# Tree attention on one core: reordered first loads, first scores and V copies

## Chip, cores, metric

One core of a Trainium2 chip. The metric is the device time of one execution in microseconds (us); the span in a profile (first to last instruction) is about 1.8 us shorter. Each kernel ran several times. A run is called fast or slow by the spread of the runs of its kernel (slow: more than 1.5% above the fastest); comparisons use fast runs where they can, and the text says where a profile is of a slow run. Ratios are the mean time of one kernel's fast runs over that of the other's of the same rounds, so they are not quite the ratios of the medians quoted beside them.

## The reference

```python
batch, heads, seq, dim = 8, 12, 512, 64
# mask[i, j] = 1 where j is i or an ancestor of i in a binary heap of 512 nodes
scores = np.einsum('bhqd,bhkd->bhqk', Q, K) / np.sqrt(dim) + (1 - mask) * (-1e9)
weights = np.exp(scores - scores.max(-1, keepdims=True))
weights = weights / (weights.sum(-1, keepdims=True) + 1e-10)
out = np.einsum('bhqk,bhkd->bhqd', weights, V)
```

The kernel computes only the tiles of the score matrix in which the mask has ones.

## The kernel before

96 heads are worked in 48 pairs. Loads come by quad (four heads, two pairs), issued from GpSimd's queue, and arrive as bf16. V is then copied into a permuted layout, one `vt` tile per octet (eight heads, four pairs): `spread_top` runs on GpSimd, `spread_l7` and `spread_leaves` on VectorE. VectorE and GpSimd run their instructions in program order in the traces here (the prediction shows a normalisation held for 7.23 us behind a copy that waits).

```python
def spread_top(o, h0=0, h1=8):        # 4 copies on GpSimd (L193)
def spread_leaves(o, r, h0=0, h1=8):  # 1 copy on VectorE (L201); r = 0, 1
def spread_l7(o, quad, h0=0, h1=8):   # 1 copy on VectorE (L213); quad = 0..3
# ... cut ...
psO = ctx.enter_context(tc.tile_pool(name="psO", bufs=1, space=bass.MemoryType.PSUM))
# ... cut ...
load(0, 2)                            # K twice, Q twice, V
load(1)
spread_top(0, 0, 4)
load(2)
spread_top(0, 4, 8)
load(3)
for i in range(2):
    transpose(i)
    evac(i)
# ... octet 0's copies on VectorE, cut ...
loaded, stored = 4, 0
for i in range(NP + 1):               # NP = 48
    q, r = divmod(i, 2)
    scores1(i)
    values(i - 1, 0)                  # guards on i cut
    scores2(i)
    values(i - 1, 1)
    norm(i - 1)                       # VectorE (L339, L340); frees the one ob tile
    transpose(i + 2)
    evac(i + 2)                       # VectorE (L253)
    o = i // 4 + 1
    if o < NQ // 2:
        if i % 4 == 0:
            spread_top(o)
        if i % 4 < 2:
            spread_l7(o, 2 * (i % 4))
            spread_l7(o, 2 * (i % 4) + 1)
        else:
            spread_leaves(o, i % 4 - 2)
    if loaded < min(NQ, q + 1 + AHEAD):
        load(loaded)
        loaded += 1
```

`values(i - 1, a)` is a run of matmuls for one head: first four that need only the top copies (L316), then two (L321) and four (L327) that need the leaves and l7 copies. They all write the tile `ob`, of which there is one. Octet `o` is first used by pair `4*o`, that is by `values` in iteration `4*o + 1`.

The softmax here doesn't subtract the row's maximum and nothing guards it: scores larger than these inputs give would overflow.

Of the kernel before, what the change touches and what calls it, by code (L numbers as in the profile page):

```python
# [34 lines left out]
def _slot_layout(t):  # L35

    found = sorted((_psum_unit(u), ROWS[kind]) for u, (kind, s) in enumerate(UNITS) if s == t)
    return [r for _, r in found], [u for u, _ in found]
# [58 lines left out]
def kernel(  # L97
# [7 lines left out]
    nc = tc.nc  # L105
    B, H, S, D = Q.shape
    P = nc.NUM_PARTITIONS
    assert S == 512 and D == 64 and P == 128 and (B * H) % 4 == 0
    scale = float(1.0 / np.sqrt(D))
    NQ = B * H // 4  # L110
    NP = 2 * NQ

    fp32 = mybir.dt.float32
    bf16 = mybir.dt.bfloat16
# [3 lines left out]
    Qr = Q.rearrange("b h (p t) d -> p (b h) (t d)", t=4)  # L118
    Kr = K.rearrange("b h (p t) d -> p (b h) (t d)", t=4)
# [9 lines left out]
    loads = ctx.enter_context(tc.tile_pool(name="loads", bufs=8))  # L129
# [34 lines left out]
    qsts, ksts, vsts = {}, {}, {}  # L164
    qTs, kTs, kqps, obs, ets, ofs = {}, {}, {}, {}, {}, {}

    def load_one(name, kept, src, q, parts=1):
        st = loads.tile([P, 4, 4, D], bf16, name=name)
        n = 4 // parts
        for j in range(parts):  # L170
            nc.gpsimd.dma_start(  # L171
                out=st[:, n * j:n * j + n, :, :].rearrange("p h t d -> p h (t d)"),
                in_=src[:, 4 * q + n * j:4 * q + n * j + n, :],
            )
        kept[q] = st

    def load_v(q):
        o, half = divmod(q, 2)
        if half == 0:
            vsts[o] = vloads.tile([P, 8, 4, D], bf16, name="vst")  # L180
        nc.gpsimd.dma_start(  # L181
            out=vsts[o][:, 4 * half:4 * half + 4, :, :].rearrange("p h t d -> p h (t d)"),
            in_=Vr[:, 4 * q:4 * q + 4, :],
        )

    def load(q, parts=1):
        load_one("kst", ksts, Kr, q, parts)
        load_one("qst", qsts, Qr, q, parts)
        load_v(q)

    def spread_top(o, h0=0, h1=8):
        for j in range(4):
            nc.gpsimd.tensor_copy(  # L193
                out=vts[o % NV][32 * j:32 * j + 32, h0:h1, 0, 0:D],
                in_=vsts[o][0:32, h0:h1, UNITS[TOP + j][1], :],
            )

    def spread_leaves(o, r, h0=0, h1=8):

        p = 64 if r else 0  # L200
        nc.vector.tensor_copy(  # L201
            out=vts[o % NV][p:p + 64, h0:h1, 1 + r:4 + r:2, 0:D],
            in_=vsts[o][64:128, h0:h1, r:3 + r:2, :],
        )

    def spread_l7(o, quad, h0=0, h1=8):

        first, slot, step = ((2, 0, 3), (2, 2, -1), (1, 3, -3), (1, 1, 1))[quad]
        src = vsts[o][32:64, h0:h1, slot, :]
        src = bass.AP(  # L210
            src.tensor, src.offset, [list(src.ap[0]), list(src.ap[1]), [step * D, 2], [1, D]]
        )
        nc.vector.tensor_copy(  # L213
            out=vts[o % NV][32 * quad:32 * quad + 32, h0:h1, first:first + 3:2, 0:D], in_=src
        )

    def transpose_one(dst, i, a, t, units, st, perm):

        step = units[1] - units[0]
        if units[2] - units[1] == step:  # L220
            dst = dst[64 * a:64 * a + 64, units[0]:units[3] + 1:step, :]
        else:
            gap = units[2] - units[0]
            dst = dst[64 * a:64 * a + 64, units[0]:units[0] + 2 * gap, :].rearrange(
                "p (x y) c -> p x y c", x=2
            )[:, :, 0:2, :]
        nc.tensor.transpose(  # L227
            out=dst, in_=st[i // 2][:, 2 * (i % 2) + a, t, :], identity=perm
        )

    def transpose(i):
        kqp = psT.tile([P, 2, 32, 32], bf16, name="kqp")
        kqps[i] = kqp
        for t in range(4):
            for a in range(2):
                transpose_one(kqp[:, 0, :, :], i, a, t, _slot_layout(t)[1], ksts, perms[t])
        for t in range(4):
            for a in range(2):
                transpose_one(
                    kqp[:, 1, :, :], i, a, t, [2 * t, 2 * t + 1, 2 * t + 9, 2 * t + 10],  # L240
                    qsts, qperm,
                )

    def evac(i):
        kq = work.tile([P, 2, 16, 32], bf16, name="kq")
        kTs[i] = kq[:, 0, :, :]
        qTs[i] = kq[:, 1, :, :].rearrange("p (t u) c -> p t (u c)", t=4)
        src = kqps[i][:, :, 0:18, :]
        src = bass.AP(
            src.tensor, src.offset,  # L250
            [list(src.ap[0]), [1024, 2], [32, 8], [9 * 32, 2], [1, 32]],
        )
        nc.vector.tensor_copy(  # L253
            out=kq[:, :, :, :].rearrange("p k (x y) c -> p k x y c", y=2), in_=src
        )
# [4 lines left out]
    def scores1(i):  # L260

        sp = psS.tile([P, 2, 512], fp32, name="s1")
        for a in range(2):
            nc.tensor.matmul(  # L264
                out=sp[:, a, :], lhsT=k1code[64 * a:64 * a + 64, :],
                rhs=q1code[64 * a:64 * a + 64, :], start=True, stop=False,
            )
        for a in range(2):
            nc.tensor.matmul(  # L269
                out=sp[:, a, :], lhsT=keys(i, a, TOP),  # L270
                rhs=qTs[i][64 * a:64 * a + 64, :, :].rearrange("p t c -> p (t c)"),
                start=False, stop=True,
            )
        et = etpool.tile([P, 2, 4, 128], bf16, name="e1")
        nc.scalar.activation(  # L275
            out=et[:, :, :, :].rearrange("p a t c -> p (a t c)"),
            in_=sp[:, :, :].rearrange("p a c -> p (a c)"),
            func=AF.Exp, scale=scale,
        )
        ets[i] = et  # L280
# [25 lines left out]
    def values(i, a):  # L306
        hh = 2 * (i % 4) + a
        if a == 0:
            obs[i] = psO.tile([P, 2, 512], fp32, name="ob")
        ob, e1, e2, vt = obs[i], ets[i], e2s[i % NE], vts[(i // 4) % NV]  # L310

        def o(t, lo=0, hi=128):
            return ob[lo:hi, a, 65 * t:65 * t + 65]

        for t in range(4):
            nc.tensor.matmul(  # L316
                out=o(t), lhsT=e1[:, a, t, :], rhs=vt[:, hh, 0, 0:D + 1],
                start=t == 0, stop=False,
            )
        for t in (2, 3):  # L320
            nc.tensor.matmul(  # L321
                out=o(t), lhsT=e2[:, a, t, :], rhs=vt[:, hh, 1 + t, 0:D + 1],
                start=False, stop=False,
            )
        for t in (0, 1):
            for lo, tile2 in ((0, SELF[t]), (64, t)):
                nc.tensor.matmul(  # L327
                    out=o(t, lo, lo + 64), lhsT=e2[:, a, t, lo:lo + 64],
                    rhs=vt[:, hh, 1 + tile2, 0:D + 1],
                    start=False, stop=t == 1,  # L330
                )
# [21 lines left out]
    AHEAD = 6  # L353
    BEHIND = 6

    load(0, 2)
    load(1)
    spread_top(0, 0, 4)
    load(2)
    spread_top(0, 4, 8)  # L360
    load(3)
    for i in range(2):
        transpose(i)
        evac(i)
    for h in (0, 4):
        for r in range(2):
            spread_leaves(0, r, h, h + 4)
        for j in range(4):
            spread_l7(0, j, h, h + 4)

    loaded, stored = 4, 0
    for i in range(NP + 1):
        q, r = divmod(i, 2)
        if i < NP:
            scores1(i)
        if 1 <= i <= NP:
            values(i - 1, 0)
        if i < NP:
            scores2(i)
        if 1 <= i <= NP:  # L380
            values(i - 1, 1)
            norm(i - 1)
        if i + 2 < NP:
            transpose(i + 2)
            evac(i + 2)
        o = i // 4 + 1
        if o < NQ // 2:
            if i % 4 == 0:
                spread_top(o)
            if i % 4 < 2:  # L390
                spread_l7(o, 2 * (i % 4))
                spread_l7(o, 2 * (i % 4) + 1)
            else:
                spread_leaves(o, i % 4 - 2)
        if loaded < min(NQ, q + 1 + AHEAD):
            load(loaded)
            loaded += 1
        behind = BEHIND if loaded < NQ else 0
        if stored < NQ - 1 and 2 * (stored + behind) + 3 <= i and (r == 1 or loaded == NQ):
            store(nc.gpsimd, stored)  # L400
            stored += 1
        if i == NP - 1:
            store(nc.sync, NQ - 1, 0, 2)
# [33 lines left out]
```

## Time and profile before

| | |
|---|---|
| median of the runs taken with the change | 161.43 us (160.22 to 163.19, 5 runs) |
| span of the profile | 159.7 us, mean granted TensorE clock 0.959 |
| first scores of pair 7 begin | 45.08 us |
| first scores of pair 47 begin | 150.25 us |
| so 40 pairs of the steady stage | 105.17 us, 2.63 each |

The start of pair 7's first scores is used below as the end of the ramp. The stretch from there to pair 47's is called the steady stage. The lines of the profile that carry the argument are in the prediction.

### The profile page before, as it was taken

The page shows a single profiled execution, that of the slowest core. Times are in us where ns is not written, and L with a number is a line of the kernel's source. Part 1 is how long each engine was busy: PE and PEld are TensorE (multiplying, and loading weights), DVE is VectorE, ACT ScalarE, POOL GpSimd, SP SyncE. Part 2 cuts the span into 40 slices and gives each one's busy share as a digit, 9 for nine tenths or more (in the row PEclk, how much of TensorE's full clock was granted, in tenths as well). Part 3 has the DMA queues.
Part 4 walks back from the last instruction along what each step waited for, and adds up shares of the span by engine and source line. Part 5 has one row for each costly group of instructions (what it writes and reads, how often), then busy time and mean ns, then how long its engine had stood idle before and what let it go on. Part 6 is the DMA issues. An engine that isn't in the chain of part 4 may idle for free.

```text
span 159.7 us, 5887 instructions
## 1 busy us (share of the span) xinstructions
PE 127.2 (80%) x2592; PEld 82.7 (52%) x2592; DVE 113.0 (71%) x229; ACT 89.0 (56%) x98; POOL 104.2 (65%) x153
## 2 busy tenths in 40 slices
PE   0378702995499899899999898999999989899860
PEld 0244301663366556565657565656657665566540
DVE  1065307671947998978889889798898998886621
ACT  3033310466046667666768576657768676567720
POOL 7839607993967979987977969669759780111010
PEclk9999999999659999999999999999999999999975
DMA  4999990999999999999999999999999999521351
GB/s 134 143 172 149 164 143 1 114 174 195 196 197 196 198 199 189 197 251 224 255 266 248 228 253 264 253 228 252 263 248 240 383 390 359 190 80 55 135 197 68
DMA packets 42090, 32.30 MB, mean 202 GB/s; under 512 B 1616, under 2 KB 38992, under 8 KB 42064
## 3 DMA queue, kind: packets, MB, share of 16 engines
q0 software_dynamic: 41360, 30.94, 109.0%
q1 hardware_dynamic: 560, 0.85, 1.6%
q8 instruction: 20, 0.33, 0.8%
q10 hardware_dynamic: 144, 0.13, 0.2%
q14 instruction: 6, 0.05, 0.1%
HBM read 38.21 MB, written 12.58 MB: 318 GB/s over the span
## 4 chain that ended last, share of the span: by engine, by line
PE 51%; DVE 19%; DMA 13%; POOL 10%; issue 4%; DVEq 0%; POOLq 0%
DMA vst<-in_V_dram 13%; PE ob L316 12%; PE ob L327 9%; PE kqp L227 8%; DVE of L340 8%; DVE vt L213 6%; PE s L286 6%; PE s L264 5%; PE s L295 4%; POOL vt L193 4%; PE s L269 4%; PE ob L321 3%; POOL kst L171 3%; POOL qst L171 3%; DVE kq L253 3%
## 5 line engine op out<-in xcount | busy, mean ns | idle before, releaser
L275 ACT ACTIVATE e<-s 128x1024 bf16<-128x1024 f32 x48 | 49.1, 1023 | 45.6 <-PE s L269 45.6
L300 ACT ACTIVATE e<-s 128x768 bf16<-128x768 f32 x48 | 38.9, 810 | 17.9 <-PE s L295 16.3
L316 PE MATMUL ob<-vt,e 128*128 128x65 bf16 x384 | 29.1, 200 | 18.2 <-DVE of L340 15.7
L193 POOL COPY vt<-vst 32x512 bf16<-32x512 bf16 (+1 forms) x52 | 31.8, 612 | 17.6 <-DMA vst<-in_V_dram 13.2
L316 PEld LDWEIGHTS <-e 128*128 128x128 bf16 x384 | 17.6, 100 | 44.9 <-DVE of L340 31.7
L253 DVE COPY kq<-kqp 128x1024 bf16<-128x1024 bf16 x48 | 32.7, 682 | 7.4 <-PE kqp L227 7.4
L213 DVE COPY vt<-vst 32x1024 bf16<-32x1024 bf16 (+1 forms) x52 | 27.2, 524 | 11.5 <-DMA vst<-in_V_dram 10.4
L340 DVE TENSOR_TENSOR of<-ob,rec 128x512 f32<-128x512 f32 x48 | 33.2, 691 | 1.7
L348 POOL DMA_DIRECT2D out_dram<-of x23 | 17.5, 761 | 22.4 <-DVE of L340 18.0
L227 PE MATMUL kqp<-ctile,kst 128*64 128x128 bf16 x384 | 20.3, 230 | 8.0 <-DMA kst<-in_K_dram 5.8
L327 PE MATMUL ob<-vt,e 128*64 128x65 bf16 x384 | 24.9, 212 | 0.0
L339 DVE RECIPROCAL rec<-ob 128x8 f32<-128x8 f32 x48 | 10.0, 208 | 19.2 <-PE ob L327 18.4
L321 PE MATMUL ob<-vt,e 128*128 128x65 bf16 x192 | 22.2, 198 | 0.0
L227 PE MATMUL kqp<-ctile,qst 128*64 128x128 bf16 x384 | 20.5, 231 | 2.0 <-DMA qst<-in_Q_dram 1.9
L171 POOL DMA_DIRECT2D qst<-in_Q_dram x25 | 19.0, 760 | 2.9 <-PE ob L316 1.7
L181 POOL DMA_DIRECT2D vst<-in_V_dram x24 | 18.6, 774 | 2.9 <-DMA vst<-in_V_dram 1.7
L171 POOL DMA_DIRECT2D kst<-in_K_dram x25 | 19.0, 759 | 2.0 <-POOLq L421 0.8
L264 PE MATMUL s<-ctile 64*128 64x512 bf16 x96 | 19.9, 409 | 0.0
L269 PE MATMUL s<-kq 64*128 64x512 bf16 x96 | 19.5, 401 | 0.0
L295 PEld LDWEIGHTS <-kq 64*128 64x128 bf16 x576 | 16.8, 97 | 3.9 <-issue 1.1
L227 PEld LDWEIGHTS <-kst 128*64 128x64 bf16 x384 | 13.7, 117 | 8.5 <-DMA kst<-in_K_dram 6.0
L295 PE MATMUL s<-kq 64*128 64x64 bf16 (+2 forms) x576 | 18.0, 193 | 0.0
(17 smaller groups left out, 88.0 us busy)
## 6 DMA issues: line engine op xcount, KB each, us to landing
out_dram<-of POOLq DMA_DIRECT2D x23, 512.0 KB, 9.5
vst<-in_V_dram POOLq DMA_DIRECT2D x24, 256.0 KB, 9.4
kst<-in_K_dram POOLq DMA_DIRECT2D x23, 256.0 KB, 8.0
qst<-in_Q_dram POOLq DMA_DIRECT2D x23, 256.0 KB, 8.6
ctile<-tree_consts SPq DMA_DIRECT2D x1, 448.0 KB, 3.1
kst<-in_K_dram POOLq DMA_DIRECT2D x2, 128.0 KB, 3.9
qst<-in_Q_dram POOLq DMA_DIRECT2D x2, 128.0 KB, 4.4
out_dram<-of SPq DMA_DIRECT2D x1, 256.0 KB, 2.2
```

The source lines that it names most:

```text
L171: nc.gpsimd.dma_start(out=st[:, n * j:n * j + n, :, :].rearrange("p h t d -> p h (t d)"), in_=src[:, 4 * q + n * j:4 * q + n * j + n, :],)
L193: nc.gpsimd.tensor_copy(out=vts[o % NV][32 * j:32 * j + 32, h0:h1, 0, 0:D], in_=vsts[o][0:32, h0:h1, UNITS[TOP + j][1], :],)
L213: nc.vector.tensor_copy(out=vts[o % NV][32 * quad:32 * quad + 32, h0:h1, first:first + 3:2, 0:D], in_=src)
L227: nc.tensor.transpose(out=dst, in_=st[i // 2][:, 2 * (i % 2) + a, t, :], identity=perm)
L253: nc.vector.tensor_copy(out=kq[:, :, :, :].rearrange("p k (x y) c -> p k x y c", y=2), in_=src)
L264: nc.tensor.matmul(out=sp[:, a, :], lhsT=k1code[64 * a:64 * a + 64, :], rhs=q1code[64 * a:64 * a + 64, :], start=True, stop=False,)
L275: nc.scalar.activation(out=et[:, :, :, :].rearrange("p a t c -> p (a t c)"), in_=sp[:, :, :].rearrange("p a c -> p (a c)"), func=AF.Exp, s ...
L295: nc.tensor.matmul(out=sp[:, a, t, lo:hi], lhsT=keys(i, a, TILE2[tile2]), rhs=qTs[i][64 * a:64 * a + 64, t, lo:hi], start=False, stop=(t, ...
L300: nc.scalar.activation(out=e2s[i % NE][:, :, :, 32:128].rearrange("p a t c -> p (a t) c"), in_=sp[:, :, :, 32:128].rearrange("p a t c -> p ...
L316: nc.tensor.matmul(out=o(t), lhsT=e1[:, a, t, :], rhs=vt[:, hh, 0, 0:D + 1], start=t == 0, stop=False,)
L327: nc.tensor.matmul(out=o(t, lo, lo + 64), lhsT=e2[:, a, t, lo:lo + 64], rhs=vt[:, hh, 1 + tile2, 0:D + 1], start=False, stop=t == 1,)
L340: nc.vector.tensor_tensor(out=ofs[q][:, 2 * r:2 * r + 2, :, :], in0=o4[:, :, :, 0:D], in1=rec[:, :, :, :].to_broadcast([P, 2, 4, D]), op=A ...
```

## The change

Its intent: the first K and Q halves and V arrive sooner, the first scores don't wait for pair 1's transposes, and octet 1's copies no longer hold up the normalisations on VectorE and the loads on GpSimd. To get that, the copies of octets 1 to 11 move two iterations later (the second leaves copy one iteration), and both leaves copies share one iteration. Core of the diff (the helper `load_one` gives way to `load_qk`, not shown):

```diff
-    load(0, 2)
+    load_qk(0, 2)                # half of K, half of Q, V, half of K, half of Q
     load(1)
     spread_top(0, 0, 4)
     load(2)
     spread_top(0, 4, 8)
-    load(3)
-    for i in range(2):
-        transpose(i)
-        evac(i)
+    transpose(0)
+    evac(0)
 ... octet 0's copies: half of them here, the other half in iterations 0 and 1
-        if i + 2 < NP:
-            transpose(i + 2)
-            evac(i + 2)
-        o = i // 4 + 1
-        if o < NQ // 2:
-            if i % 4 == 0:
-                spread_top(o)
-            if i % 4 < 2: ...two spread_l7
-            else:
-                spread_leaves(o, i % 4 - 2)
-        if loaded < min(NQ, q + 1 + AHEAD):
+        for n in ([1, 2] if i == 0 else [i + 2]):
+            if n < NP:
+                transpose(n)
+                evac(n)
+        o = (i - 2) // 4 + 1
+        step = (i - 2) % 4
+        if i >= 2 and o < NQ // 2 and step == 0:
+            ...spread_top(o), by halves for o == 1
+        if loaded < min(NQ, i + 4, q + 1 + AHEAD):
             load(loaded)
             loaded += 1
+        if i >= 2 and o < NQ // 2:
+            if step < 2: ...two spread_l7
+            elif step == 2:
+                spread_leaves(o, 0)
+                spread_leaves(o, 1)
```

In the changed kernel the lines are numbered four higher: L197 are GpSimd's top copies, L205 the leaves, L217 the l7 copies, L257 the evacuation, L320, L325 and L331 the value matmuls, L343 and L344 the normalisation.

More of the change, by code (lines that the diff above doesn't have):

```diff
@@ L165 @@
     qTs, kTs, kqps, obs, ets, ofs = {}, {}, {}, {}, {}, {}
-    def load_one(name, kept, src, q, parts=1):
-        st = loads.tile([P, 4, 4, D], bf16, name=name)
-        n = 4 // parts
-        for j in range(parts):
-            nc.gpsimd.dma_start(
-                out=st[:, n * j:n * j + n, :, :].rearrange("p h t d -> p h (t d)"),
-                in_=src[:, 4 * q + n * j:4 * q + n * j + n, :],
-            )
-        kept[q] = st
     def load_v(q):
@@ L184, in load_v, with load, load_qk @@
         )
-    def load(q, parts=1):
-        load_one("kst", ksts, Kr, q, parts)
-        load_one("qst", qsts, Qr, q, parts)
+    def load(q):
+        load_qk(q, 1)
         load_v(q)
+    def load_qk(q, parts):
+        pairs = []
+        for name, kept, src in (("kst", ksts, Kr), ("qst", qsts, Qr)):
+            kept[q] = loads.tile([P, 4, 4, D], bf16, name=name)
+            pairs.append((kept[q], src))
+        n = 4 // parts
+        for j in range(parts):
+            for st, src in pairs:
+                nc.gpsimd.dma_start(
+                    out=st[:, n * j:n * j + n, :, :].rearrange("p h t d -> p h (t d)"),
+                    in_=src[:, 4 * q + n * j:4 * q + n * j + n, :],
+                )
+            if j == 0 and parts > 1:
+                load_v(q)
     def spread_top(o, h0=0, h1=8):
@@ L360 @@
     spread_top(0, 4, 8)
-    load(3)
-    for i in range(2):
-        transpose(i)
-        evac(i)
-    for h in (0, 4):
-        for r in range(2):
-            spread_leaves(0, r, h, h + 4)
-        for j in range(4):
-            spread_l7(0, j, h, h + 4)
-    loaded, stored = 4, 0
+    loaded, stored = 3, 0
+    transpose(0)
+    evac(0)
+    for r in range(2):
+        spread_leaves(0, r, 0, 4)
+    for j in range(4):
+        spread_l7(0, j, 0, 4)
     for i in range(NP + 1):
@@ L382 @@
             norm(i - 1)
-        if i + 2 < NP:
-            transpose(i + 2)
-            evac(i + 2)
-        o = i // 4 + 1
-        if o < NQ // 2:
-            if i % 4 == 0:
-                spread_top(o)
-            if i % 4 < 2:
-                spread_l7(o, 2 * (i % 4))
-                spread_l7(o, 2 * (i % 4) + 1)
-            else:
-                spread_leaves(o, i % 4 - 2)
-        if loaded < min(NQ, q + 1 + AHEAD):
+        for n in ([1, 2] if i == 0 else [i + 2]):
[5 more added lines that the diff above has]
+        if i >= 2 and o < NQ // 2 and step == 0:
+            if o == 1:
+                spread_top(o, 0, 4)
+                spread_top(o, 4, 8)
+            else:
+                spread_top(o)
+        if loaded < min(NQ, i + 4, q + 1 + AHEAD):
             load(loaded)
             loaded += 1
+        if i == 0:
+            for r0 in range(2):
+                spread_leaves(0, r0, 4, 8)
+        if i == 1:
+            for j in range(4):
+                spread_l7(0, j, 4, 8)
+        if i >= 2 and o < NQ // 2:
+            if step < 2:
+                spread_l7(o, 2 * step)
+                spread_l7(o, 2 * step + 1)
+            elif step == 2:
+                spread_leaves(o, 0)
+                spread_leaves(o, 1)
         behind = BEHIND if loaded < NQ else 0
```

## The prediction

> **What bounds the kernel now.** The work is 48 pairs of heads. K, Q and V come in groups of four heads (a quad, two pairs: 256 KB each of K, Q and V after the cast), and V is copied into its layout by eight heads (an octet, two quads, four pairs). I read the page first: TensorE 80% busy, VectorE 71%, but one slice of 40 in which DMA moves 1 GB/s. So I looked for stages, not for one bound, with the table of stretches:
>
> ```profile
> core 0: us, PE busy (x) PEld busy (x) DVE busy (x) ACT busy (x) POOL busy (x), PEclk, DMA share, GB/s
> 0.00:19.56 19.56, 10.37 (x124) 6.01 (x124) 7.37 (x22) 5.04 (x6) 13.96 (x26) 1.00 1.09 152
> 19.56:26.84 7.28, 0.00 (x0) 0.00 (x0) 2.10 (x5) 1.02 (x1) 2.04 (x3) 1.00 0.68 89
> ...
> 38.36:42.08 3.72, 0.00 (x0) 0.00 (x1) 2.54 (x5) 1.02 (x1) 2.48 (x4) 0.83 1.45 196
> ...
> 51.50:133.00 81.50, 76.60 (x1681) 50.40 (x1680) 71.97 (x142) 56.73 (x63) 65.50 (x93) 1.00 1.34 253
> ```
>
> TensorE does nothing for 7.3 us from 19.56 and for 3.7 us from 38.36; from 51.5 to 133 it is 94% busy. The steady stage is TensorE's (with VectorE close behind); the losses are in the ramp. The timeline says what ends both stalls (start, duration, what ran, then the idle before it and its releaser):
>
> ```profile
> 14.49 1.77 POOL L193 COPY vt<-vst 32x256 bf16<-32x256 bf16 x4
> 16.20 0.81 POOL L171 DMA_DIRECT2D kst<-in_K_dram  x1
> 17.00 0.76 POOL L171 DMA_DIRECT2D qst<-in_Q_dram  x1
> 17.73 0.77 POOL L181 DMA_DIRECT2D vst<-in_V_dram  x1
> ...
> 24.66 1.16 DVE L213 COPY vt<-vst 32x1024 bf16<-32x1024 bf16 x2 [7.23 <-DMA vst<-in_V_dram]
> 24.69 2.94 POOL L193 COPY vt<-vst 32x512 bf16<-32x512 bf16 x4 [6.18 <-DMA vst<-in_V_dram]
> 25.85 0.21 DVE L339 RECIPROCAL rec<-ob 128x8 f32<-128x8 f32 x1
> 26.10 0.69 DVE L340 TENSOR_TENSOR of<-ob,rec 128x512 f32<-128x512 f32 x1
> 26.85 0.40 PE L316 MATMUL ob<-vt,e 128*128 128x65 bf16 x4 [7.33 <-DVE of L340]
> 27.58 0.74 POOL L171 DMA_DIRECT2D kst<-in_K_dram  x1
> ...
> 39.46 1.59 DVE L213 COPY vt<-vst 32x1024 bf16<-32x1024 bf16 x2 [3.20 <-DMA vst<-in_V_dram]
> ...
> 42.08 0.40 PE L316 MATMUL ob<-vt,e 128*128 128x65 bf16 x4 [3.82 <-DVE of L340]
> ```
>
> Two in-order queues do the harm. On VectorE, octet 1's copies (L213) stand in pair 0's iteration, ahead of pair 0's normalisation (L339, L340); they wait for V of quad 3 until 24.66, and only the normalisation frees the one PSUM tile into which the next pair's value matmuls go. On GpSimd, octet 1's top copies (L193) stand ahead of the loads of quad 4, so no load is issued from 18.5 to 27.58 and the DMA runs dry. That late start makes V of quad 5 land only at 39.46: the second stall. The chain of waits agrees:
>
> ```profile
> 17.73 6.83 DMA vst<-in_V_dram
> 24.69 0.86 POOL vt L193
> ...
> 31.40 7.97 DMA vst<-in_V_dram
> 39.46 0.84 DVE vt L213
> ```
>
> **What the Trainium skill says.** "Perfetto Trace Analysis", DMA Instruction — SWDGE: the profiled window of a GpSimd-issued DMA ends when descriptors are written, not when data has moved. The trace agrees: 0.76 us per issue, 8.0 to 9.4 us to landing on the page. "DMA: Bandwidth & Descriptors", Anatomy of one DMA: about 2.0 us fixed plus bytes over 436 GB/s, and semaphore waits happen on the issuing sequencer. For 256 KB that is an estimate of 2.6 us; the trace has 6 us and more, because several loads share the engines, so I use the trace. The second half is what the two queues show: a GpSimd instruction that waits holds back every DMA behind it. "SBUF — State Buffer", Who interferes with whom: a VectorE copy in a two-port mode and a GpSimd instruction exclude each other. The trace fits: an L213 copy takes 0.42 us alone, and up to 0.84 us while L193 runs. "TensorE: Matmul & The Clock Gate", Part 1: after some 3.4 us of idleness matmuls run at half clock until as much work has passed. Here four L316 matmuls take 0.40 us after each stall and 0.29 us later, although the clock column does not always show it.
>
> **The change part by part.** The data and arithmetic are unchanged. GpSimd gets 4 more copies for octet 1, now in half octets; VectorE's copies keep their number and size. What changes is order.
>
> 1. First loads. Before: K twice, Q twice, V. After: first half of K, first half of Q, V, then the other halves. The first half of Q is issued at about 2.0 instead of 2.8. Landings before lie on a line: K's half (0.131 MB) is used at 5.26 and V of quad 1 (1.573 MB in all) at 14.36: 1.442 MB in 9.1 us, 158 GB/s. So Q's half, with 0.262 MB, lands at 5.26 + 0.131/0.158 = 6.1 instead of 7.06, and V0, with 0.524 MB, at about 7.8 to 8.5 instead of 10.38. First scores, no longer behind pair 1's transposes: 6.1 + 0.6 transposes + 0.7 evacuation, about 7.6 instead of 9.48. This 1.9 us is not kept: pair 2's transposes still wait for Q of quad 1, which is bytes-bound at 12.7 to 13.06.
>
> 2. GpSimd goes on 2 us earlier after V0, so quad 2's loads are issued at about 10 instead of 12.15, and the dip in DMA rate at 12 to 14.5 closes. That brings V of quad 3 from 24.66 to about 23.3.
>
> 3. Octet 1's top copies now come behind quad 4's loads, octet 1's VectorE copies behind norm(1) and the evacuation of pair 4. When VectorE blocks on V of quad 3, norms 0 and 1 are done. So TensorE blocks at values of pair 3, not pair 1. It resumes at 23.3 + 1.3 (two L213 beside GpSimd) + 0.9 (norm) = 25.5. Before, the value matmuls of pair 3 began at 33.21. Gain: 7.7 us.
>
> 4. Quad 4 is issued at about 18.5 to 20.7, before the DMA runs dry. Before, the stretch 24.7 to 30.5 moved 34 GB/s against 197 when full, which loses 5.8 x (1 - 34/197) = 4.8 us. With item 2 and the slow restart the DMA is some 7 us earlier. V of quad 5 then lands at 39.46 - 7 = 32.5. It is needed in iteration 6. From 25.5, VectorE has a backlog, so I give iterations 4 to 6 about 3.3 us each: pair 6's scores at about 33, and VectorE reaches octet 2's copies at about 37. No wait: the second stall of 3.7 us goes.
>
> Pair 7's scores start at 45.08 before; after, at about 33 + 3 = 36. Gain up to there: 9 us. It is 2.4 less than 7.7 + 3.7 because the backlog of octet 1 is worked off in those iterations.
>
> 5. Steady stage. Before, pair 7 to pair 47 takes 150.25 - 45.08 = 105.2 us, 2.63 a pair. The two L201 copies now stand in one iteration (about 0.42 to 0.56 each), none in the next. VectorE per iteration is 0.24 + 0.61 + 0.71 = 1.56 plus copies; 1.0 gives 2.56, against TensorE's period of 2.51. The trace shows a copy time of 1.2 to 1.4 costs TensorE 0.46 and 0.84 costs almost nothing (VectorE still waits 0.18 there). So 1.0 costs about 0.1, eleven octets about 1 us, at most 1.7. I take 0.7.
>
> The tail (last norm 155.67 to 159.7) is the same: last stores and the end.
>
> Sum: -9 + 0.7 = -8.3 us. The run profiled took 161.52, the three timed ones 160.22, 163.02 and 163.19, mean 162.1. So 162.1 - 8.3 = 153.8; I say 153.5.
>
> **The rivals.** A: the DMA becomes the bound. From 51.5 to 133 it is full already (share 1.34, 253 GB/s), and a quad costs 0.786/197 = 4.0 us of loads plus about 1.3 of a store at 390 GB/s, 5.3 us, against TensorE's 5.2. TensorE moves up 9 us, the DMA only 7. The close spot is the pool of 9 output tiles: store 9 is issued at 112.69 and takes 10, so it lands at 122.9; the tile is needed at 126.6. 3.7 us of slack, less 2, should hold. If not, the gain is that of the DMA or a little more, 5 to 7 us, and the time 155 to 157. Against it: after 133 the DMA is mostly idle (share 0.45), and no load is waited for after 42.
> B: V of quad 3 lands no earlier (24 to 24.7) and VectorE's backlog is dearer: the L213 copies run beside eight top copies. Then pair 7 starts at 38 to 39: gain 6, time about 156.
> C: everything overlaps better, V of quad 3 lands at 22 as the queue stays deep (the DMA does 197 GB/s with a deep queue, 158 in the ramp), and shorter idleness spares TensorE's slow clock (0.40 against 0.29 for four matmuls). Gain 11 to 12, time 150 to 151.
> D: the stall merely moves, since V is needed just as much. For it: V of quad 3 is bytes-bound, 3.1 MB at some 150 GB/s. Against it: pairs 1 and 2 are done before it, and the DMA does not run dry. Under D the time stays at 160 or more.
>
> **Range and chances.** The main sum has errors of about 1.5 us in V's landing, 1.5 in the backlog, 1 in the steady stage, and the runs of one kernel differ by 3 us. 8 in 10: 150 to 157.5. Over 2% faster means under 159.8, which only D misses: 0.93. Within 2%: 0.06. Slower: 0.01.
>
> **What would show it.** Right: no GpSimd gap of 6 us between 18 and 25; no slice near 1 GB/s; one TensorE stall of 3 to 5 us ending near 25.5 at value matmuls, none near 38; pair 7's scores near 36; then 2.6 a pair. Wrong: normalisations waiting on stores' DMA (A), a long L213 wait past 33 (the DMA shift is too small), or a steady pair over 2.65 (item 5 too small).

## The result, and the profile after

The change took 173.51 us (median of 5, 171.56 to 176.73) against 161.43: ratio 1.0708, 95% interval 1.0608 to 1.0807. It is slower, and outside the predicted range. The profile taken is of a slow run (span 175.0, clock 0.885; fast runs had a clock of 0.92 to 0.93). The same kernel (change_again; expected 171.5 to 173.5 us in fast runs) gave a ratio of 1.0635: fast runs of 171.51 and 172.46, slow ones of 174.82 and 175.42, its profile again of a slow one. It was run at another time.

The ramp did what was hoped. First, TensorE's waits in the timeline of the changed kernel (start, duration, what ran, idle before it and its releaser):

```profile
26.54 0.40 PE L320 MATMUL ob<-vt,e 128*128 128x65 bf16 x4 [3.31 <-DVE of L344]
31.10 0.21 PE L325 MATMUL ob<-vt,e 128*128 128x65 bf16 x1 [0.20 <-DVE vt L205]
31.84 0.22 PE L325 MATMUL ob<-vt,e 128*128 128x65 bf16 x1 [0.53 <-DVE vt L205]
40.95 0.29 PE L320 MATMUL ob<-vt,e 128*128 128x65 bf16 x4 [0.36 <-DVE of L344]
44.48 0.19 PE L325 MATMUL ob<-vt,e 128*128 128x65 bf16 x1 [0.66 <-DVE vt L205]
45.02 0.19 PE L325 MATMUL ob<-vt,e 128*128 128x65 bf16 x1 [0.35 <-DVE vt L205]
```

One stall of 3.3 us is left, ending at 26.54; the stall of 7.3 and the one near 42 are gone. Pair 7 begins at 37.40, 7.7 us sooner than before. But at 31 and at 44.5 there is something new: L325 waits for the leaves copies (L205), at the first pair of octet 1 and of octet 2. It goes on to the end. Two lines from the view of waits of the changed kernel (us in total, times, longest) show it; VectorE's wait for the value matmuls was 18.4 us before, and the second line the kernel before does not have at all:

```profile
DVE rec L343 <- PE ob L331: 41.7, 27, 2.2
...
PE ob L325 <- DVE vt L205: 12.4, 21, 0.9
```

Here is one octet boundary from the timeline of the changed kernel, pair 12 being the first of octet 3:

```profile
54.23 0.39 PE L268 MATMUL s<-ctile 64*128 64x512 bf16 x2
54.38 0.21 DVE L343 RECIPROCAL rec<-ob 128x8 f32<-128x8 f32 x1
...
54.62 0.69 DVE L344 TENSOR_TENSOR of<-ob,rec 128x512 f32<-128x512 f32 x1
...
55.23 0.68 DVE L257 COPY kq<-kqp 128x1024 bf16<-128x1024 bf16 x1
55.46 0.28 PE L320 MATMUL ob<-vt,e 128*128 128x65 bf16 x4 [0.62 <-DVE of L344]
55.92 1.11 DVE L205 COPY vt<-vst 64x1024 bf16<-64x1024 bf16 x2
...
56.45 0.19 PE L325 MATMUL ob<-vt,e 128*128 128x65 bf16 x1 [0.71 <-DVE vt L205]
...
57.08 0.19 PE L325 MATMUL ob<-vt,e 128*128 128x65 bf16 x1 [0.44 <-DVE vt L205]
...
58.43 0.21 DVE L343 RECIPROCAL rec<-ob 128x8 f32<-128x8 f32 x1 [1.40 <-PE ob L331]
```

Read it as a chain. The normalisation frees `ob` and the first four value matmuls go (55.46). The next two need the leaves copies, and on VectorE these stand behind the evacuation: 0.68 plus 1.11 us. Then VectorE in turn idles 1.40 us until the value matmuls are through. Neither engine is short of capacity; for one pair in four they take turns. The same place in the timeline of the kernel before, pair 28 being the first of octet 7:

```profile
102.33 0.42 DVE L201 COPY vt<-vst 64x1024 bf16<-64x1024 bf16 x1
...
103.52 0.69 DVE L340 TENSOR_TENSOR of<-ob,rec 128x512 f32<-128x512 f32 x1
...
104.13 0.68 DVE L253 COPY kq<-kqp 128x1024 bf16<-128x1024 bf16 x1
...
104.36 0.28 PE L316 MATMUL ob<-vt,e 128*128 128x65 bf16 x4
104.48 0.22 PE L321 MATMUL ob<-vt,e 128*128 128x65 bf16 x2
```

There the last leaves copy is ahead of the normalisation for which TensorE must wait anyway, so TensorE does not wait for it.

What four pairs cost in the changed kernel is in the table of stretches (columns as in the prediction: stretch, length, busy time of each engine, then clock, DMA share, GB/s). The stretches run from pair 10 to 14 and from pair 14 to 18:

```profile
46.71:58.77 12.06, 10.14 (x221) 6.53 (x218) 9.33 (x19) 7.33 (x9) 10.26 (x16) 1.00 1.45 196
58.77:72.05 13.28, 11.13 (x220) 7.26 (x218) 10.05 (x19) 7.28 (x9) 10.13 (x15) 0.91 1.39 234
```

Before, four pairs took 10.5 us (4 x 2.63). At the full clock they take 12.06 now, with a lowered one 13.28. So there are two losses: a wait, and a clock. A closer look at the second boundary, again the table of stretches, from the value matmuls on:

```profile
67.50:69.50 2.00, 0.53 (x6) 0.31 (x6) 1.84 (x3) 0.54 (x1) 2.00 (x4) 1.00 1.44 197
69.50:71.00 1.50, 1.50 (x27) 1.04 (x28) 0.00 (x0) 0.33 (x1) 1.10 (x2) 0.59 1.43 231
71.00:72.50 1.50, 1.50 (x25) 1.00 (x24) 1.16 (x3) 0.48 (x1) 0.78 (x2) 0.50 1.17 328
```

TensorE is busy for 0.53 of 2.00 us, and then runs for 3 us at about half the clock.

Over the whole steady stage (pair 7 to 47): 128.2 us against 105.2, 23.0 more, in this slow run; the ramp gave 7.7 back.

### The profile page after: what moved, and what is told of

It reads as the page before. It is cut to its first block, busy times and chain, and to the rows that moved or that the text cites. A ratio compares the mean times of both kernels' runs of the same rounds, so it can differ in the third digit from the quotient of the medians.

```text
span 175.0 us, 5898 instructions
## 1 busy us (share of the span) xinstructions
PE 139.1 (79%) x2592; PEld 87.8 (50%) x2592; DVE 113.7 (65%) x229; ACT 89.0 (51%) x98; POOL 104.6 (60%) x157
## 4 chain that ended last, share of the span: by engine, by line
PE 41%; DVE 34%; DMA 14%; POOL 5%; issue 4%; DVEq 0%; POOLq 0%
DVE of L344 10%; PE ob L320 8%; DMA vst<-in_V_dram 8%; PE ob L331 7%; DVE kq L257 7%; DVE vt L217 7%; DVE vt L205 7%; DMA qst<-in_Q_dram 6%; PE s L290 6%; PE kqp L231 6%; PE s L299 4%; PE s L268 4%; PE ob L325 3%; DVE rec L343 3%; PE s L273 3%
## 5 line engine op out<-in xcount | busy, mean ns | idle before, releaser
L320 PE MATMUL ob<-vt,e 128*128 128x65 bf16 x384 | 30.4, 206 | 10.8 <-DVE of L344 9.2
L320 PEld LDWEIGHTS <-e 128*128 128x128 bf16 x384 | 18.4, 103 | 40.0 <-DVE of L344 19.4
L197 POOL COPY vt<-vst 32x512 bf16<-32x512 bf16 (+1 forms) x56 | 32.1, 573 | 10.1 <-DMA vst<-in_V_dram 5.2
L343 DVE RECIPROCAL rec<-ob 128x8 f32<-128x8 f32 x48 | 9.9, 207 | 42.8 <-PE ob L331 41.7
L257 DVE COPY kq<-kqp 128x1024 bf16<-128x1024 bf16 x48 | 32.7, 681 | 7.3 <-PE kqp L231 7.2
L325 PE MATMUL ob<-vt,e 128*128 128x65 bf16 x192 | 24.7, 204 | 13.1 <-DVE vt L205 12.4
L344 DVE TENSOR_TENSOR of<-ob,rec 128x512 f32<-128x512 f32 x48 | 33.2, 691 | 1.7
L217 DVE COPY vt<-vst 32x1024 bf16<-32x1024 bf16 (+1 forms) x52 | 26.2, 505 | 4.2 <-DMA vst<-in_V_dram 3.1
L231 PE MATMUL kqp<-ctile,kst 128*64 128x128 bf16 x384 | 21.4, 240 | 6.3 <-DMA kst<-in_K_dram 5.2
L331 PE MATMUL ob<-vt,e 128*64 128x65 bf16 x384 | 25.6, 217 | 0.0
L231 PE MATMUL kqp<-ctile,qst 128*64 128x128 bf16 x384 | 21.8, 243 | 1.2 <-DMA qst<-in_Q_dram 1.2
L273 PE MATMUL s<-kq 64*128 64x512 bf16 x96 | 21.2, 439 | 0.3 <-DVE kq L257 0.3
L268 PE MATMUL s<-ctile 64*128 64x512 bf16 x96 | 21.2, 438 | 0.0
L331 PEld LDWEIGHTS <-e 128*64 128x64 bf16 x384 | 14.3, 114 | 12.7 <-issue 7.4
L171 POOL DMA_DIRECT2D vst<-in_V_dram x24 | 18.4, 765 | 3.9 <-DVE of L344 1.2
L299 PE MATMUL s<-kq 64*128 64x64 bf16 (+2 forms) x576 | 18.8, 198 | 0.0
```

What stands on the lines that cost most here:

```text
L197: nc.gpsimd.tensor_copy(out=vts[o % NV][32 * j:32 * j + 32, h0:h1, 0, 0:D], in_=vsts[o][0:32, h0:h1, UNITS[TOP + j][1], :],)
L217: nc.vector.tensor_copy(out=vts[o % NV][32 * quad:32 * quad + 32, h0:h1, first:first + 3:2, 0:D], in_=src)
L231: nc.tensor.transpose(out=dst, in_=st[i // 2][:, 2 * (i % 2) + a, t, :], identity=perm)
L257: nc.vector.tensor_copy(out=kq[:, :, :, :].rearrange("p k (x y) c -> p k x y c", y=2), in_=src)
L299: nc.tensor.matmul(out=sp[:, a, t, lo:hi], lhsT=keys(i, a, TILE2[tile2]), rhs=qTs[i][64 * a:64 * a + 64, t, lo:hi], start=False, stop=(t, ...
L320: nc.tensor.matmul(out=o(t), lhsT=e1[:, a, t, :], rhs=vt[:, hh, 0, 0:D + 1], start=t == 0, stop=False,)
```

## The experiments

Theories: **T1**, a deadline: the last copies of each octet stand right ahead of their first use, and TensorE waits for them. **T2**: two leaves copies in one iteration are too much for VectorE, wherever they stand. **T3**: the earlier ramp makes TensorE outrun the DMA, or changes its clock. All kernels gave correct results. All profiles but the two of the change are of fast runs. Baselines are 160.73 (runs a, b, c, p), 161.40 (d, f, t, g), 161.57 (the change again, k, s, v). They were run at other times.

| run | median us | ratio to before | pair 7 begins | pairs 7 to 47 | clock in it |
|---|---|---|---|---|---|
| before | 161.4 | 1 | 45.1 | 105.2 | 0.99 |
| the change (slow profile) | 173.51 | 1.071 | 37.4 | 128.2 | 0.91 |
| the change again (slow profile) | 173.64 | 1.064 | 35.3 | 128.4 | 0.89 |
| a_copies_back | 154.71 | 0.956 | 37.6 | 104.5 | 1.00 |
| b_late_alone | 178.66 | 1.110 | 41.1 | 126.3 | 0.92 |
| c_one_earlier | 155.72 | 0.969 | 37.5 | 108.2 | 0.98 |
| p_gpsimd_late | 156.16 | 0.974 | 36.0 | 109.4 | 0.98 |
| v_vector_late | 175.13 | 1.085 | 37.7 | 123.6 | 0.93 |
| d_leaves_first | 159.28 | 0.986 | 34.7 | 113.4 | 0.98 |
| s_scores_first | 165.14 | 1.021 | 37.8 | 117.5 | 0.96 |
| k_fill_gap2 | 166.34 | 1.027 | 35.6 | 119.8 | 1.00 |
| f_old_start | 155.65 | 0.968 | 38.1 | 106.5 | 1.00 |
| t_top_early | 156.32 | 0.971 | 33.9 | 111.2 | 0.95 |
| g_halves | 149.74 | 0.929 | 31.3 | 107.9 | 1.00 |

The 95% intervals are within about 0.01 of each ratio. Single profiles scatter in the ramp: the change had pair 7 at 37.40 and, run again, at 35.31.

The view of waits gives TensorE's wait for the leaves copies (L325 for L205) in each profile. The sum for a_copies_back:

```profile
PE ob L325 <- DVE vt L205: 1.5, 3, 0.6
```

It is 12.4 and 12.7 us in the two profiles of the change, 11.1 in b (there L321 for L201), 9.9 in v and 11.5 in s; 5.0 in d and 4.8 in k; 0.9 to 1.9 in c, p, f and t; and g has none.

### Is it the ramp or the place of the copies: a and b

a_copies_back keeps the ramp of the change, and moves the copies of octets 3 to 11 back (octet 2's stay late):

```diff
-        o = (i - 2) // 4 + 1
-        step = (i - 2) % 4
+        back = 2 if i < 9 else 1 if i < 12 else 0
+        o = (i - back) // 4 + 1
+        step = (i - back) % 4
 ...
             elif step == 2:
                 spread_leaves(o, 0)
-                spread_leaves(o, 1)
+                if back:
+                    spread_leaves(o, 1)
+            elif not back:
+                spread_leaves(o, 1)
```

> The ramp of the change, but from octet 4 on the V copies of both engines stand where they stood before (octet 3 one iteration nearer). Theory T1 (deadline: the last copies of an octet now stand in the iteration right ahead of its first value matmuls, so TensorE waits for them once per octet): the loss of the steady stage goes, the gain of the ramp (7.7 us at pair 7) stays, about 154 us. Theory T2 (two L205 copies in one iteration are too much for VectorE): about 154 too. Theory T3 (the earlier ramp makes TensorE outrun the DMA or lowers its clock, wherever the copies stand): 165 to 172 us.

Measured 154.71 (153.11 to 156.4; two of the four runs were slow, the fast ones are 153.11 and 153.62), ratio 0.9564. The steady stage is that of the kernel before, 104.5 us, with the new ramp. T3 falls. The table of stretches for its steady stage:

```profile
37.60:142.12 104.52, 98.59 (x2148) 64.61 (x2144) 89.52 (x179) 72.60 (x80) 75.70 (x106) 1.00 1.25 241
```

b_late_alone is the reverse: the kernel before, ramp and loads as they were, with only the copies of octets 2 to 11 late:

```diff
-        o = i // 4 + 1
-        if o < NQ // 2:
+        back = 0 if i < 4 else 2
+        o = (i - back) // 4 + 1
+        step = (i - back) % 4
+        if o < NQ // 2 and i not in (4, 5):
 ... i % 4 becomes step; both leaves at step 2 when back is 2
```

> The kernel before, ramp and first loads untouched, with only the copies of octets 2 to 11 two iterations later and both L201 copies in one iteration, as in the change. T1 and T2: the steady loss of some 1.6 to 2 us per octet shows without the new ramp: 161.4 + 10 x 1.8, less up to 3 for the second stall: 173 to 179 us. T3: 159 to 163 us.

178.66, ratio 1.1104: the loss shows without any of the new start. It even gained 4 us in the ramp (the second stall is gone, since octet 2's copies wait two iterations later for their V) and lost 21.1 in the steady stage.

### Deadline or load on VectorE: c

c_one_earlier keeps the grouping of the change, two, two, two, none, and gives it one iteration more:

```diff
+        back = 2 if i < 9 else 1
-        o = (i - 2) // 4 + 1
-        step = (i - 2) % 4
+        o = (i - back) // 4 + 1
+        step = (i - back) % 4
```

> The change, with the copies of octets 3 to 11 one iteration earlier and still grouped two, two, two, none. It parts T1 from T2: the grouping on VectorE is the same, only the last copies now have one iteration to spare. T1: 153 to 157 us. T2: 168 to 173 us, as the change. T3: 165 to 172 us.

155.72. T2 predicted 168 or more and falls; T1 stands. The grouping may cost a little: the steady stage is 108.2 against 104.5 in a_copies_back, at a clock of 0.98 against 1.00.

### Which engine's copies: p and v

p_gpsimd_late is a_copies_back with GpSimd's top copies still late (they keep `i - 2`); v_vector_late is the change with GpSimd's top copies moved back and VectorE's still late.

```diff
 p:  spread_top placed by i - 2; VectorE's copies placed by i - back, leaves as in a_copies_back
 v:  spread_top placed by i - back; VectorE's copies placed by i - 2
```

> As a_copies_back, but GpSimd's top copies stay two iterations later, as in the change; only VectorE's copies are moved back. T1 with VectorE's copies alone as the cause: the same as a_copies_back within 1 us, about 154. If GpSimd's late copies cost anything (by meeting VectorE's copies, or by being late themselves): 157 us or more.

156.16: by the medians 1.5 us over a_copies_back, so between my two cases; by the fast runs of the two, 2.8 us (156.2 against 153.4), so nearer to the second. The steady stage is 4.9 us longer, and the view of groups names where VectorE's time goes. For a_copies_back (count, then busy us and mean ns of one):

```profile
L217 DVE COPY vt<-vst 32x1024 bf16<-32x1024 bf16 (+1 forms) x52 | 24.8, 477 | 4.4 <-DMA vst<-in_V_dram 3.4
```

and for p_gpsimd_late:

```profile
L217 DVE COPY vt<-vst 32x1024 bf16<-32x1024 bf16 (+1 forms) x52 | 30.0, 577 | 4.5 <-DMA vst<-in_V_dram 3.4
```

The same 52 copies take 100 ns more each, 5.2 us. They now meet GpSimd's copies more often; this is the likely cause, though only the durations are shown.

> The complement of p_gpsimd_late: the change, but from octet 4 on GpSimd's top copies stand where they stood before; VectorE's copies stay late. If VectorE's place is nearly all of the loss: 169.5 to 172.5 us, about 1.3 below the change at most (p_gpsimd_late was 1.3 over a_copies_back). If the loss needs both to be late: under 165 us.

175.13, above the range I gave. Two of the four runs were slow; the two fast ones, 172.06 and 174.41, lie with the change's own 171.51 and 172.46. Moving GpSimd's copies back repaired nothing. Whether it cost something can't be told from these runs. VectorE's place is the cause; GpSimd's late copies cost something in p, where VectorE's are in time (the expectation's 1.3 us for it is 1.5 by the medians, 2.8 by the fast runs).

### What the chain is made of: d and s

d_leaves_first leaves both copies in the last iteration, but ahead of its evacuation:

```diff
+        if i >= 2 and o < NQ // 2 and step == 2:
+            spread_leaves(o, 0)
+            spread_leaves(o, 1)
         for n in ([1, 2] if i == 0 else [i + 2]):
             if n < NP:
                 transpose(n)
                 evac(n)
```

> The change, with the two L205 copies of an octet still in the iteration right ahead of their first use, but issued ahead of that iteration's evacuation (0.68 us) instead of behind it. T1 (TensorE waits for norm, then evacuation, then both copies): the evacuation leaves the chain, 10 octets x 0.7 us come back, 163 to 167 us, against 171.6 to 173.5 of the change. If the wait is not this chain but VectorE's total work or the clock alone: 170 to 173 us.

159.28, better than I expected. The boundary in its timeline:

```profile
51.76 0.69 DVE L344 TENSOR_TENSOR of<-ob,rec 128x512 f32<-128x512 f32 x1
...
52.48 0.88 DVE L205 COPY vt<-vst 64x1024 bf16<-64x1024 bf16 x2
52.60 0.28 PE L320 MATMUL ob<-vt,e 128*128 128x65 bf16 x4 [0.32 <-DVE of L344]
52.96 0.19 PE L325 MATMUL ob<-vt,e 128*128 128x65 bf16 x1
53.39 0.69 DVE L257 COPY kq<-kqp 128x1024 bf16<-128x1024 bf16 x1
53.41 0.19 PE L325 MATMUL ob<-vt,e 128*128 128x65 bf16 x1 [0.27 <-DVE vt L205]
```

The waits of 0.71 and 0.44 became none and 0.27. Nine of the ten octets of this trace (four pairs each, from pair 6) ran at clock 1.00 and took 11.32 us on average, against 12.06 in the changed kernel's octet at clock 1.00: 0.7 per octet, 7 us over ten, as I had counted for the evacuation. The fast runs of the two differ by 13.1 us (158.9 against 172.0); the other 6 us fit the clock (0.98 in the steady stage), which I had left out, and which k_fill_gap2 measures.

s_scores_first keeps VectorE's order and lets TensorE do the next second scores ahead of the first value matmuls of an octet:

```diff
+        first = i >= 9 and i % 4 == 1
+        if first:
+            scores2(i)
         if 1 <= i <= NP:
             values(i - 1, 0)
-        if i < NP:
+        if i < NP and not first:
             scores2(i)
```

> The change, with the second scores of the next pair (about 0.5 us of TensorE) issued ahead of the first value matmuls of each octet from octet 2 on, so that useful work fills part of the wait. T1 says TensorE waits at the value matmuls for a chain that is longer by evacuation and two copies than usual, about 1.6 us per octet; 0.5 us of it is then used: 10 x 0.5 = 5 us less, plus some clock: 163 to 167.5 us. If the iteration is bound by VectorE's work and not by this wait: 171 us or more.

165.14, in the expected range, and 6.8 us under the change by the fast runs (165.15 against 171.99). Its five octets at clock 1.00 took 11.4 us against 12.06, so some 6 us are direct. The wait of L325 for L205 itself hardly shrank (11.5 us): the leaves copies come no sooner. What shrank is the work behind them: at the boundary of octet 3 VectorE waits 0.94 us for the value matmuls instead of 1.40. So TensorE's work behind the copies is a link of the chain, as T1 has it.

### The clock: k

k_fill_gap2 is the change plus repeats of the mask matmuls of the second scores, which start their tile anew and so change nothing, placed in the wait:

```diff
             nc.tensor.matmul(
                 out=o(t), lhsT=e1[:, a, t, :], rhs=vt[:, hh, 0, 0:D + 1],
                 start=t == 0, stop=False,
             )
+        if a == 0 and i % 4 == 0 and i >= 8:
+            for _ in range(4):
+                mask2(i + 1, True)    # the two mask matmuls of scores2(i + 1)
```

> The change, with four idempotent repeats of the mask matmuls of the second scores (8 matmuls of 384 columns) put into TensorE's wait for the L205 copies, once per octet from octet 2 on. They fill the wait and do nothing else. If the lowered clock (0.92 to 0.93 in the change's fast runs) comes from these idle gaps: clock 0.96 or more, and the time falls by 2 to 5 us to 167 to 170, the direct wait of some 1.6 us per octet staying. If the clock has another cause: clock 0.93 and 172 to 174 us.

166.34, a little under the 167 to 170 expected, with a clock of 0.957 to 0.98 over whole runs, and 1.00 in the steady stage:

```profile
35.63:155.46 119.83, 108.46 (x2229) 68.31 (x2226) 92.50 (x179) 72.77 (x81) 76.86 (x109) 1.00 1.11 214
```

Eighty matmuls that do nothing made the kernel faster. The fast runs average 166.05 against 171.99 for the change (171.51 and 172.46): 5.9 us of its loss is the clock, and it comes from the idle gaps at the octet boundaries. The fill cost nothing itself: all octets of this trace ran at clock 1.00, and those from pair 10 to 46 took 12.06 us on average, as the change's octet at 1.00. The rest of the way to the fast runs of a_copies_back (153.11 and 153.62, mean 153.4) is 12.7 us; that run moves the copies of nine octets, so 1.4 us each. This is a remainder, and a_copies_back moves GpSimd's copies too, so not all of it need be the direct wait for the leaves. The traces agree roughly: an octet takes 12.06 against 10.37 in a_copies_back (pairs 10 to 46), 1.7 us, and the waits of L325 for L205 are 12.4 us against 1.5, 10.9 less.

### What the parts of the ramp are worth: f, t and g

f_old_start is a_copies_back with the old first loads and first transposes:

```diff
-        for j in range(parts):
-            for st, src in pairs:
+        for st, src in pairs:
+            for j in range(parts):
 ... V behind all four; transpose and evac of pairs 0 and 1 ahead of the loop
```

> a_copies_back with the first loads and first transposes as before: both halves of K, both of Q, then V; pairs 0 and 1 transposed ahead of the first scores. The prediction said that the 1.9 us earlier first scores are not kept and that an earlier V0 brings V of quad 3 by about 1.4 us: so 1 to 2 us over a_copies_back (154.7), 155.5 to 156.5. If the first loads are the main gain of the ramp: 159 us or more. If they are worth nothing: 154.5.

155.65, in the expected range: by the medians some 1 us over a_copies_back (half of whose runs were slow), by the ratios 0.9679 - 0.9564 of 161, 1.9 us. First scores began at 9.74 instead of 7.30 there, second ones at 13.77 instead of 13.52: the earlier first scores are mostly not kept.

t_top_early is a_copies_back with octet 1's top copies on GpSimd ahead of quad 4's loads again:

```diff
+        if i == 1:
+            spread_top(1)
-        if i >= 2 and o < NQ // 2 and step == 0: ...by halves for o == 1
+        if i >= 3 and o < NQ // 2 and step == 0:
+            spread_top(o)
```

> a_copies_back, but octet 1's top copies on GpSimd stand ahead of quad 4's loads again. My reading is that this is what dried up the DMA: it should come back, V of quad 5 some 5 us later, and a stall of 2 to 4 us at octet 2's first copies: 157 to 159 us. If only the order on VectorE mattered: 154 to 155 us.

156.32, less than the 157 to 159 that I expected; by the ratios it is 2.3 us over a_copies_back (0.9708 - 0.9564 of 161). The mechanism is there: one slice of the page again shows 0 GB/s. Lines of its timeline:

```profile
22.76 1.16 DVE L217 COPY vt<-vst 32x1024 bf16<-32x1024 bf16 x2 [1.42 <-DMA vst<-in_V_dram]
...
38.84 0.84 DVE L217 COPY vt<-vst 32x1024 bf16<-32x1024 bf16 x2 [3.76 <-DMA vst<-in_V_dram]
...
40.70 0.40 PE L320 MATMUL ob<-vt,e 128*128 128x65 bf16 x4 [3.70 <-DVE of L344]
```

The stall at octet 2 is back, 3.7 us. But with no loads of quad 4 behind it, V of quad 3 is there at 22.76 instead of 24.67 in a_copies_back and 24.36 in the change, so part of the loss is gained earlier. Part of it shows only behind the stall: from 40.70 to 48.37 the clock is 0.50, and t_top_early, 0.8 us behind a_copies_back at pair 9 (43.71 against 42.87), is 2.5 us behind at pair 14 (59.60 against 57.15). The kernel before is at 64.31 there. The larger part of the ramp's gain is thus the order on VectorE together with the first loads.

g_halves uses what the others showed. Octets 1 and 2 are copied by halves of four heads, each half as its own quad of V lands, and none in the last iteration ahead of its use; the rest is a_copies_back:

```diff
-            if o == 1:
-                spread_top(o, 0, 4)
-                spread_top(o, 4, 8)
+        if i in (2, 4):
+            spread_top(1, 2 * i - 4, 2 * i)
 ...
+        for oo in (1, 2):
+            k = i - 4 * oo + 2
+            h = 2 * (k // 2 * 2)
+            if k in (0, 2):
+                for j in range(4):
+                    spread_l7(oo, j, h, h + 4)
+            elif k in (1, 3):
+                for r0 in range(2):
+                    spread_leaves(oo, r0, h, h + 4)
-        if i >= 2 and o < NQ // 2:
+        if i >= 9 and o < NQ // 2:
```

> a_copies_back, but octets 1 and 2 are copied by halves of four heads: the first half two to three iterations ahead of its use, the second half two iterations behind it, as V of its own quad lands; none stands in the iteration right ahead of its first use. The stall at V of quad 3 (TensorE 3.55 us, ending at 26.85) and the wait at octet 2's first use (0.64 + 0.55 us and what follows) should shrink to under 1 us: 150 to 152.5 us. If the bytes of K and Q bound the ramp anyway: 153.5 to 155 us.

149.74 (149.34 to 150.17; expected 150 to 152.5), ratio 0.9291: 7% faster than the kernel before, and faster than anything else here. Pair 7 begins at 31.33, and TensorE's longest wait for a normalisation is 1.3 us, against 4.0 in a_copies_back. Its steady stage, 107.9, is 3.4 us longer than that of a_copies_back; why was not tried. Its view of waits has one line that no other run's has: normalisations (L344) wait for the DMA of a store, 5 times, 1.2 us in all, so the output tiles, rival A's close spot, begin to matter here.

## Why the prediction was wrong

What made the prediction wrong was one term, item 5, the steady stage. The prediction said: "So 1.0 costs about 0.1, eleven octets about 1 us, at most 1.7. I take 0.7." It took the two leaves copies as load on VectorE, and read the price of a copy from places of the trace where TensorE waits for the normalisation behind the copy (0.46 us at 99.25) and no matmul waits for the copy's result. It did not ask which matmuls read the result and how soon. In the change they are the value matmuls of the very next iteration. In place of 0.7 us the runs showed 18.6 us between the fast runs of the change and of a_copies_back: 5.9 us of lowered clock (k_fill_gap2) and 12.7 us besides, most of it the wait of the value matmuls for the leaves copies (10.9 us less of it in a_copies_back). Deadline, not load: c_one_earlier has the same load and takes 155.72. The answer was in the code: octet `o` is first used in iteration `4*o + 1`, and the change puts its last copies into iteration `4*o`.

The other steps, in order:

- Item 1, first loads: right. First scores at 7.09 (7.6 predicted); not kept; f_old_start puts the whole start at about 1.9 us by the ratios.
- Item 2, V of quad 3 at 23.3: it was 24.36, only 0.3 earlier than before. The DMA did not dip at 12 us, but then it had quad 4's loads to serve as well. Rival B's first half was right.
- Item 3, resumption at 25.5: 26.54, and at value matmuls of pair 3, as said.
- Item 4, no second stall, and pair 7 at about 36: no second stall, pair 7 at 37.40 and 35.31 in the two profiles. Right, with some luck, as V came 1.1 us later than the sum assumed; and t_top_early shows GpSimd's order to be worth some 2.3 us, less than the second stall's 3.7.
- Rival A, the DMA as the bound: did not come with the change. Normalisations wait for a store's DMA only in the profile of g_halves, 1.2 us in all.
- The range: with item 5 at nothing, a_copies_back took 154.71 (153.4 in its fast runs), against 153.5 predicted. The rest of the sum was right within its errors.
- The list of signs named the right one: "a steady pair over 2.65 (item 5 too small)". It is 3.2 in the slow profile (128.2 / 40), and still 3.0 at clock 1.00 (12.06 / 4).
- The chances: slower was given 0.01, because the rivals concerned the ramp and the DMA. None concerned the place of the copies in the stage in which the kernel spends two thirds of its time and which every moved line of the loop also changes.

## What to carry to other kernels

When a change moves work later in a loop, write down for each moved instruction the first instruction that reads its result and count what lies between, on both engines; a copy that was free can become a link of the chain without becoming longer. Fix a ramp in the ramp: give the first iterations their own placement and leave the steady loop alone, as a_copies_back and g_halves do. When TensorE waits in short gaps, look at the clock of the stretch behind each gap: here it cost 5.9 us on top of 12.7.

## What the Trainium skill lacked or had wrong

- "TensorE: Matmul & The Clock Gate", HAM oscillation: its rule is to have no idle gaps over some 3.4 us. Here much shorter gaps (0.81 and 0.55 us, with TensorE busy 0.53 of 2.00 us around them) were followed by 3 us at a clock of 0.50 to 0.59, and filling the gaps with matmuls that do nothing brought back 5.9 us. At another boundary (0.71 and 0.44 us) the clock stayed at 1.00, so these runs give no threshold either. The page mentions micro-idles in a section on PSUM-queue cycling, without a threshold; it lacks one for partly busy windows.
- "DMA: Bandwidth & Descriptors", Anatomy of one DMA: the fit of 2.0 us plus bytes over 436 GB/s is not the time to landing when several loads share the queue. Here 256 KB took 8.5 to 9.7 us to landing in the changed kernel (median by kind), where an estimate by the fit is 2.6. The page has no figure for how loads queued behind delay one that is ahead: V of quad 3 was there at 22.76 without quad 4's loads behind it, and at 24.36 and 24.67 with them (single profiles).
- "SBUF — State Buffer", Who interferes with whom: it tells which copies exclude each other and gives slowdowns of single measurements, but not what that costs a stream of copies. Here moving GpSimd's copies two iterations raised the mean of 52 VectorE copies from 477 to 577 ns; that they meet more often is inferred.
